# Seven products in place of eight for half of the gate and up projections of a hybrid layer's two feed-forward stages

## The chip, the cores and the metric

The kernel runs on one core of a Trainium2 chip. The time is the device time of one execution in microseconds. Everything is float32 from outside; inside, each operand is split into a high and a low part (fp32r), and a product of two such operands is three matmuls (high by high, high by low, low by high), so that the result keeps float32's precision.

## The reference

One layer of an encoder trunk, on 256 tokens of width 2048: a feed-forward stage, a mixer (retention and a state-space part in parallel) and a second feed-forward stage, each with a scaled residual and a layer norm behind it. The change touches the two feed-forward stages:

```
D_FF = 5632
def swiglu_ffn(x, w_gate, w_up, w_down):
    return (jax.nn.silu(x @ w_gate) * (x @ w_up)) @ w_down

x = layer_norm(DEEPNORM_ALPHA * x + 0.5 * swiglu_ffn(x, ffn1...), ln1_gain, ln1_bias)
mix = hybrid_mixer(x, ...)
x = layer_norm(DEEPNORM_ALPHA * x + mix, ln2_gain, ln2_bias)
x = layer_norm(DEEPNORM_ALPHA * x + 0.5 * swiglu_ffn(x, ffn2...), ln3_gain, ln3_bias)
```

## The kernel before

The 256 tokens are two tiles of 128 (t = 0, 1), the width of 2048 is 16 blocks of 128 (k). Each feed-forward stage has 11 column tiles of 512 (`NH`), j = 0 to 10. For each, `ffn` runs the gate projection and then the up projection: `proj` (line 164) takes four weight units of 1 MB (128x2048, four blocks of k by 512 columns), and for each k and t `mm_t` (line 114) issues three matmuls of 128x512 into a PSUM bank of that t. So a unit is 24 matmuls, and a column tile 2 x 4 x 24 = 192. `gated` (line 237) makes silu(gate) times up times 0.5 (two activations on ScalarE, two operations on VectorE), and `turn` (line 248) transposes the result on TensorE (8 small matmuls) and splits it for the down projection. The down projection (`down`, line 267) comes in chunks of 4, 4 and 3 column tiles (`CHUNKS`): for each of four output tiles n, all units of the chunk go into two banks, which `add_res` (line 262) adds to the residual rows `res` in SBUF. The last chunk ends in the layer norm (`LN.close`).

A weight unit goes through `wparts` (line 91): SP's queue loads `raw`, ScalarE casts it to the high part `hi`, VectorE subtracts to get the low part `lo`. There are 4 buffers for `hi`, 4 for `lo` and 3 for `raw`, and they set how far loads run ahead: a load waits until VectorE has read the raw buffer that it takes.

The first column tile of the first stage (lines 177 to 210) loads tokens and gate and up units together, in smaller pieces, since all of them start cold. The first gate tile of the second stage is run inside the closing of the layer norm before it.

The order in which each engine gets its instructions is set by the framework's scheduler, which works from a timeline of its own; only within the layer norms' closes is the program's order kept (`strict`). `page` (line 56) hands out 27 tiles of 128x512 for activations (`NPG`), `tmp` 12 of 128x256. `rope_tables` (line 521) makes the rotary tables; the scheduler puts its instructions at the program's start.

## Time and profile before

| | |
|---|---|
| median of 3 runs | 1921.06 us (1919.58 to 1921.64) |
| the profiled execution | 1921.3 us |
| its span | 1919.5 us |
| TensorE busy | 1885.5 us, 98% |
| VectorE busy | 1046.7 us, 55% |
| ScalarE busy | 778.2 us, 41% |
| GpSimd busy | 60.9 us, 3% |
| mean granted TensorE clock | 0.995 |
| DMA | 363.07 MB, mean 189 GB/s |

PE is TensorE, PEld its weight loads, DVE VectorE, ACT ScalarE, POOL GpSimd, SP SyncE, which issues the weight loads. The span runs from the first to the last event of the profile; the execution's own time is 1.8 us longer. In the names of tiles, h and l ahead of a weight's name are its high and low part and r is the raw load; f1 and f2 are the two stages, then g, u, d with the numbers of column tile and unit.

### The profile page before, as it was taken

To read this page: it belongs to the slowest core of one execution; us is meant where nothing else is said; L and a number is where in the kernel's file an instruction comes from. 1 tells how busy PE (TensorE), PEld (TensorE's weight loads), DVE (VectorE), ACT (ScalarE), POOL (GpSimd) and SP (SyncE) were. 2 spreads that over 40 slices of the span, in tenths; PEclk is the share of its full clock that TensorE was granted. 3 is DMA by queue.
4 is the path that set the end of the run, shared out by engine and by line. 5 is a ranking of instruction groups with operands and counts; after the bars stand their busy time and mean duration, and the time that the engine had idled before them with its cause. 6 is when DMAs were issued, how large, how long until landed. Compare 5 with 4: busy or idle time off the path is not lost.

```text
span 1919.5 us, 20769 instructions
## 1 busy us (share of the span) xinstructions
PE 1885.5 (98%) x8722; PEld 1566.5 (82%) x8722; DVE 1046.7 (55%) x1044; ACT 778.2 (41%) x672; POOL 60.9 (3%) x72
## 2 busy tenths in 40 slices
PE   8999999999999998999999998999999999999997
PEld 6888888888888887888888886888888888888885
DVE  6444445444444455867867645644445444444456
ACT  5433333433333336653335437433433343333331
POOL 3000000000000000002300000000000000000000
PEclk9999999999999999999999999999999999999999
DMA  8655555555555553544345554555555555556551
GB/s 331 217 186 195 189 187 194 194 183 194 197 192 200 206 200 137 215 174 160 132 156 190 197 198 142 214 187 187 196 194 188 188 198 184 188 197 234 184 196 66
DMA packets 53581, 363.07 MB, mean 189 GB/s; under 512 B 6240, under 2 KB 6512, under 8 KB 10992
## 3 DMA queue, kind: packets, MB, share of 16 engines
q1 hardware_dynamic: 49536, 350.25, 50.8%
q0 software_dynamic: 2656, 9.41, 1.4%
q10 hardware_dynamic: 1296, 2.10, 0.3%
q8 instruction: 68, 1.11, 0.2%
q14 instruction: 25, 0.20, 0.0%
HBM read 359.63 MB, written 2.10 MB: 188 GB/s over the span
## 4 chain that ended last, share of the span: by engine, by line
PE 95%; ACT 2%; DVE 2%; DMA 1%; issue 0%; POOL 0%; SPq 0%; DVEq 0%
PE f2u L78 12%; PE f1g L78 11%; PE f2g L78 11%; PE f1u L78 11%; PE f1d_p L78 9%; PE f2d_p L78 9%; PE opp L78 4%; PE xb L78 3%; PE f1dz_p L78 3%; PE f2dz_p L78 3%; PE g L78 2%; PE z L78 2%; PE first L78 1%; PE v L78 1%; PE v0e L78 1%; DVE res L78 1%
## 5 line engine op out<-in xcount | busy, mean ns | idle before, releaser
L78 PE MATMUL f2u<-hf2u,l2x 128*128 128x512 f32 x704 | 218.8, 389 | 0.0
L78 PE MATMUL f1g<-hf1g,x 128*128 128x512 f32 x640 | 201.5, 391 | 0.0
L78 PE MATMUL f2g<-hf2g,l2x 128*128 128x512 f32 x640 | 201.2, 391 | 0.0
L78 PE MATMUL f1u<-hf1u,x 128*128 128x512 f32 x640 | 198.6, 389 | 0.0
L78 DVE TENSOR_TENSOR lf2u<-rf2u,hf2u 128x2048 fp32r<-128x2048 f32 x44 | 100.9, 2292 | 125.2 <-ACT hf2u L78 125.2
L78 DVE TENSOR_TENSOR lf1u<-rf1u,hf1u 128x2048 fp32r<-128x2048 f32 x40 | 91.7, 2292 | 122.3 <-ACT hf1u L78 122.3
L78 PEld LDWEIGHTS f2u<-hf2u,l2x 128*128 128x128 f32 x704 | 132.1, 188 | 27.3
L78 DVE TENSOR_TENSOR lf1g<-rf1g,hf1g 128x2048 fp32r<-128x2048 f32 x40 | 91.6, 2292 | 101.5 <-ACT hf1g L78 101.5
L78 DVE TENSOR_TENSOR lf2g<-rf2g,hf2g 128x2048 fp32r<-128x2048 f32 x40 | 91.6, 2292 | 98.7 <-ACT hf2g L78 98.7
L78 PEld LDWEIGHTS f1u<-hf1u,x 128*128 128x128 f32 x640 | 120.1, 188 | 24.9
L78 PEld LDWEIGHTS f1g<-hf1g,x 128*128 128x128 f32 x640 | 120.2, 188 | 24.8
L78 PEld LDWEIGHTS f2g<-hf2g,l2x 128*128 128x128 f32 x640 | 120.1, 188 | 24.6
L78 PE MATMUL f2u<-lf2u,l2x 128*128 128x512 f32 x352 | 137.0, 389 | 0.2 <-DVE lf2u L78 0.2
L78 ACT CAST hf2g<-rf2g 128x2048 fp32r<-128x2048 f32 x40 | 76.5, 1913 | 131.4 <-PE f2u L78 98.9
L78 ACT CAST hf2u<-rf2u 128x2048 fp32r<-128x2048 f32 x44 | 84.1, 1911 | 110.6 <-PE f2g L78 104.7
L78 ACT CAST hf1g<-rf1g 128x2048 fp32r<-128x2048 f32 x40 | 76.4, 1913 | 125.0 <-PE f1u L78 95.3
L78 PE MATMUL f1g<-lf1g,x 128*128 128x512 f32 x320 | 124.6, 389 | 0.0
L78 PE MATMUL f2g<-lf2g,l2x 128*128 128x512 f32 x320 | 124.6, 389 | 0.0
L78 PE MATMUL f1u<-lf1u,x 128*128 128x512 f32 x320 | 124.5, 389 | 0.0
L78 DVE TENSOR_TENSOR lf2d<-rf2d,hf2d 128x2048 fp32r<-128x2048 f32 x32 | 73.4, 2293 | 85.6 <-ACT hf2d L78 85.6
L78 DVE TENSOR_TENSOR lf1d<-rf1d,hf1d 128x2048 fp32r<-128x2048 f32 x32 | 73.4, 2293 | 85.6 <-ACT hf1d L78 85.6
L78 ACT CAST hf1u<-rf1u 128x2048 fp32r<-128x2048 f32 x40 | 76.4, 1910 | 106.3 <-PE f1g L78 105.5
(797 smaller groups left out, 3846.4 us busy)
## 6 DMA issues: line engine op xcount, KB each, us to landing
rf2u<-f_u SPq DMA_DIRECT2D x44, 1024.0 KB, 4.8
rf1g<-f_g SPq DMA_DIRECT2D x40, 1024.0 KB, 4.8
rf1u<-f_u SPq DMA_DIRECT2D x40, 1024.0 KB, 4.8
rf2g<-f_g SPq DMA_DIRECT2D x40, 1024.0 KB, 4.8
rf1d<-f_d SPq DMA_DIRECT2D x32, 1024.0 KB, 4.8
rf2d<-f_d SPq DMA_DIRECT2D x32, 1024.0 KB, 4.8
rop<-wout SPq DMA_DIRECT2D x16, 1024.0 KB, 4.8
rf1dz<-f_d SPq DMA_DIRECT2D x12, 1024.0 KB, 4.8
```

The lines of the kernel that those rows point to most:

```text
L78: ins = fn(*args, **kw)
```

## The change

For column tiles 1 to 10 of each stage (20 of 22), the first half of the inner dimension (units 0 and 1 of gate and up, 16 k blocks of which 8) is computed by Strassen's scheme in Winograd's form. The 2 x 2 blocks are: two token tiles by two k halves of the activations (a11, a12, a21, a22) and two k halves by gate and up of the weights (g1, g2, u1, u2). Seven products, each 4 blocks of k by three matmuls = 12 matmuls, take the place of eight. `forms` makes the four combinations of activations once per stage: 12 operations of VectorE and 4 casts on ScalarE, each 128x512. `fused` makes the four sums of weights (u1-g1, u1-u2 kept as u2-u1, u2-g1, g2-u2) per tile on VectorE as 128x2048 operations, and splits seven weight operands in place of four; the other half (units 2 and 3) stays as it was. Four copies on ScalarE keep intermediate sums of a PSUM bank, because bank x goes on accumulating: the first product, then the fourth (t2), then the fifth (t3).

The down projection of tiles 0 to 7 no longer goes by chunks: `rows_at` runs it for one column tile at a time, a unit of 24 matmuls for each n, and the four units stand between the products of the next tile (`more()`). Each unit is added to the residual by itself. Tiles 9 and 10 have no down units between their products; the last down projection has tiles 8, 9 and 10 as before.

Memory: `raw` and `lo` share 6 buffers (4 + 3 before), the Strassen loads have 4 of their own ("sr"), `NPG` is 19, and there is a pool per stage (`phase`) which holds `tmp`, the Strassen loads or the convolution's pages (`page2`). `rope_tables` moves ahead of the first stage in the text. The last layer norm's rows come in two wide loads of 128x2048 in place of eight of 128x512.

```diff
-CHUNKS = [(0, 4), (4, 4), (8, 3)]
+LASTC = 8
-NPG = 27
+NPG = 19
...
+    def page2(name, dt=F32, shape=(P, 512)):
+        return phase["pool"].tile(list(shape), dt, tag="pm", name=name, bufs=9)
...
     def wparts(src, name, k, c):
         n = k * c
         hi = wpool.tile([P, D], F32R, tag="whi", name="h" + name, bufs=4)
-        lo = wpool.tile([P, D], F32R, tag="wlo", name="l" + name, bufs=4)
-        raw = wpool.tile([P, D], F32, tag="raw", name="r" + name, bufs=3)
+        lo = wpool.tile([P, D], F32R, tag="wrl", name="l" + name, bufs=6)
+        raw = wpool.tile([P, D], F32, tag="wrl", name="r" + name, bufs=6)
...
+    cs = const.tile([P, 2, T], F32, name="cs")
+
+    def rope_tables():
...
+    rope_tables()
...
+                r = 2 * self.idx + i
+                src = aps["lnr"][r:r + 1, :]
+                if self.nxt is None:
+                    g = phase["pool"].tile([P, D], F32, tag="sr", name=f"{self.name}gb{i}", bufs=4)
+                    nc.gpsimd.dma_start(out=g, in_=src.broadcast_to([P, D]))
+                    self.gb.append([g[:, n * NS:(n + 1) * NS] for n in range(4)])
+                    continue
                 row = []
                 for n in range(4):
                     g = page(f"{self.name}gb{i}{n}")
-                    r = 2 * self.idx + i
-                    nc.gpsimd.dma_start(
-                        out=g, in_=aps["lnr"][r:r + 1, n * NS:(n + 1) * NS].broadcast_to([P, NS]))
+                    nc.gpsimd.dma_start(out=g, in_=src[:, n * NS:(n + 1) * NS].broadcast_to([P, NS]))
...
-    def ffn(act, which, ln, psg, psu=None):
+    def forms(x4, name):
+        r = {}
+        for q in range(2):
+            for t in range(2):
+                v = page(f"{name}r{q}{t}", F32, (P, 4, P))
+                sl = slice(t * P, (t + 1) * P)
+                vec.tensor_tensor(out=v, in0=x4[q][:, :, 0, sl].bitcast(F32), in1=x4[q][:, :, 1, sl].bitcast(F32),
+                                  op=ALU.add)
+                r[q, t] = v
+        a11, a21, a12, a22 = r[0, 0], r[0, 1], r[1, 0], r[1, 1]
+        vec.tensor_tensor(out=a22, in0=a21, in1=a22, op=ALU.add)
+        vec.tensor_tensor(out=a21, in0=a11, in1=a21, op=ALU.subtract)
+        vec.tensor_tensor(out=a11, in0=a22, in1=a11, op=ALU.subtract)
+        vec.tensor_tensor(out=a12, in0=a12, in1=a11, op=ALU.subtract)
+        out = []
+        for i, v in enumerate((a22, a11, a21, a12)):
+            hi = page(f"{name}sh{i}", F32R, (P, 4, P))
+            lo = page(f"{name}sl{i}", F32R, (P, 4, P))
+            split(v, hi, lo)
+            out.append(lambda k, hi=hi, lo=lo: (hi[:, k, :], lo[:, k, :]))
+        return out
+
+    def ffn(act, x4, which, ln, psg, psu=None):
         wg, wu, wd = aps[f"{which}_g"], aps[f"{which}_u"], aps[f"{which}_d"]
         todo = []
 
@@ -472,31 +547,129 @@
         def run(src, name):
             got = None
             for i, ps in enumerate(proj(src, act, name)):
-                if i == 0:
-                    flush()
                 got = ps
             return got
 
-        pend = None
-        for ci, (j0, nj) in enumerate(CHUNKS):
-            hs = []
-            for j in range(j0, j0 + nj):
-                if psg is None:
-                    psg = run(wg[j], f"{which}g{j}")
-                if psu is None:
-                    psu = run(wu[j], f"{which}u{j}")
-                toks = gated(psg, psu, f"{which}t{j}")
-                todo.append(lambda toks=toks, j=j, hs=hs: turn(toks, f"{which}t{j}", hs))
-                psg = psu = None
-                if pend is not None:
-                    pend()
-                    pend = None
-
-            def pend(hs=hs, nj=nj, j0=j0, ci=ci):
-                down(lambda n, u: wd[n, j0 + u], hs, nj, f"{which}d{ci}_", ci == 0)
+        if psu is None:
+            psu = run(wu[0], f"{which}u0")
+        s1f, s2f, s3f, s4f = forms(x4, which)
+
+        def raw_of(q, t):
+            return lambda k: act[4 * q + k](t)
+
+        def rows_at(j, n, hs):
+            pss = [bank(f"{which}d{j}p{n}{t}") for t in range(2)]
+            w = wunit(wd[n, j], f"{which}d{j}_{n}", 4, NS)
+            for k in range(4):
+                for t in range(2):
+                    mm_t(pss[t], hs[k], t, w, k, k == 0, k == 3)
+            for t in range(2):
+                add_res(pss[t], t, n, j == 0)
+
+        def fused(j, rest):
+            name = f"{which}s{j}"
+            fx = phase["pool"]
+
+            def load(src, nm):
+                t = fx.tile([P, D], F32, tag="sr", name=f"{name}{nm}", bufs=4)
+                nc.sync.dma_start(out=t, in_=src)
+                return t
+
+            def parts(v, nm):
+                hi = wpool.tile([P, D], F32R, tag="whi", name=f"{name}h{nm}", bufs=4)
+                lo = wpool.tile([P, D], F32R, tag="wrl", name=f"{name}l{nm}", bufs=6)
+                split(v, hi, lo)
+                return hi.rearrange("p (k c) -> p k c", c=NS), lo.rearrange("p (k c) -> p k c", c=NS)
+
+            def prod(ps, fm, w, first, last):
+                for k in range(4):
+                    ah, al = fm(k)
+                    ten.matmul(ps, lhsT=ah, rhs=w[0][:, k, :], start=first and k == 0, stop=False, skip_group_check=True)
+                    ten.matmul(ps, lhsT=ah, rhs=w[1][:, k, :], start=False, stop=False, skip_group_check=True)
+                    ten.matmul(ps, lhsT=al, rhs=w[0][:, k, :], start=False, stop=last and k == 3, skip_group_check=True)
+
+            def plain(src, kc, nm, banks, first, last):
+                w = wunit(src[kc], f"{name}{nm}{kc}", 4, NS)
+                for k in range(4):
+                    for t in range(2):
+                        ah, al = act[4 * kc + k](t)
+                        ps = banks[t]
+                        ten.matmul(ps, lhsT=ah, rhs=w[0][:, k, :], start=first and k == 0, stop=False, skip_group_check=True)
+                        ten.matmul(ps, lhsT=ah, rhs=w[1][:, k, :], start=False, stop=False, skip_group_check=True)
+                        ten.matmul(ps, lhsT=al, rhs=w[0][:, k, :], start=False, stop=last and k == 3, skip_group_check=True)
+
+            def more():
+                if rest:
+                    rest.pop(0)()
+
+            def sub(o, a, b):
+                vec.tensor_tensor(out=o, in0=a, in1=b, op=ALU.subtract)
+
+            def snap(ps, nm):
+                v = page(f"{name}{nm}")
+                sca.copy(out=v, in_=ps)
+                return v
+
+            def plus(v, ps):
+                vec.tensor_tensor(out=v, in0=ps, in1=v, op=ALU.add)
+
+            g1 = load(wg[j, 0], "g1")
+            u1 = load(wu[j, 0], "u1")
+            x = bank(name + "x")
+            prod(x, raw_of(0, 0), parts(g1, "g1"), True, True)
+            c11 = snap(x, "c11")
+            b1 = [bank(f"{name}b{t}1") for t in range(2)]
+            plain(wg[j], 2, "g", b1, True, False)
+            u2 = load(wu[j, 1], "u2")
+            sub(g1, u1, g1)
+            yb = bank(name + "y")
+            prod(yb, s1f, parts(g1, "t1"), True, True)
+            c22 = snap(yb, "c22")
+            flush()
+            plain(wg[j], 3, "g", b1, False, False)
+            g2 = load(wg[j, 1], "g2")
+            more()
+            b12 = bank(name + "b12")
+            prod(b12, s4f, parts(u2, "u2"), True, False)
+            sub(u1, u2, u1)
+            sub(u2, u2, g1)
+            prod(x, s2f, parts(u2, "t2"), False, True)
+            c12 = snap(x, "c12")
+            vec.tensor_tensor(out=c12, in0=c12, in1=c22, op=ALU.add)
+            more()
+            prod(x, s3f, parts(u1, "t3"), False, True)
+            c21 = snap(x, "c21")
+            prod(b1[0], raw_of(1, 0), parts(g2, "g2"), False, True)
+            plus(c11, b1[0])
+            sca.activation(c11, c11, AF.Silu)
+            more()
+            sub(g2, g2, u2)
+            prod(b1[1], raw_of(1, 1), parts(g2, "t4"), False, True)
+            plus(c21, b1[1])
+            sca.activation(c21, c21, AF.Silu)
+            plain(wu[j], 2, "u", [b12, x], False, False)
+            more()
+            plain(wu[j], 3, "u", [b12, x], False, True)
+            plus(c12, b12)
+            plus(c22, x)
+            for a, u in ((c11, c12), (c21, c22)):
+                vec.scalar_tensor_tensor(out=a, in0=u, scalar=0.5, in1=a, op0=ALU.mult, op1=ALU.mult)
+            return [c11, c21]
+
+        hs = []
+        toks = gated(psg, psu, f"{which}t0")
+        todo.append(lambda toks=toks, hs=hs: turn(toks, f"{which}t0", hs))
+        rest = [lambda n=n, hs=hs: rows_at(0, n, hs) for n in range(4)]
+        tail = []
+        for j in range(1, NH):
+            toks = fused(j, rest)
+            hs = [] if j <= LASTC else hs
+            todo.append(lambda toks=toks, j=j, hs=hs: turn(toks, f"{which}t{j}", hs))
+            if j < LASTC:
+                rest = [lambda n=n, j=j, hs=hs: rows_at(j, n, hs) for n in range(4)]
         if ln.nxt is None:
             ln.affine()
-        return down(lambda n, u: wd[n, j0 + u], hs, nj, f"{which}dz_", False, ln, flush)
+        return down(lambda n, u: wd[n, LASTC + u], hs, NH - LASTC, f"{which}dz_", False, ln, flush)
 
...
-    ps1 = ffn(act0, "f1", ln1, first_ps[0], first_ps[1])
-    ps2 = mixer(ln1.x, ps1, ln2)
-    ffn([halves(a) for a in ln2.x], "f2", LN(2, "l3"), ps2)
+    with tc.tile_pool(name="fx1", bufs=1) as phase["pool"]:
+        ps1 = ffn(act0, x0_4, "f1", ln1, first_ps[0], first_ps[1])
+    with tc.tile_pool(name="mx", bufs=1) as phase["pool"]:
+        ps2 = mixer(ln1.x, ps1, ln2)
+    with tc.tile_pool(name="fx2", bufs=1) as phase["pool"]:
+        ffn([halves(a) for a in ln2.x], ln2.x4, "f2", LN(2, "l3"), ps2)
```

Three places show what the new order is; the names are f1s4 for the Strassen tile 4 of the first stage (x, y, b01, b11, b12 its banks; c11 to c22 its copies; ht2 and lt2 the parts of u2-g1, ht3 and lt3 those of u2-u1), f1d3_0 to f1d3_3 for the four down units of column tile 3, which stand between its products, and f1t3 for that tile's transposed result.

ScalarE before, in the gate and up units of tile 5, where the casts alternate with little else:

```order
L78 CAST hf1g53_2119<-rf1g53_2121 128x2048 [waits DMAHW0_49,DVE_49,PE_49]
L78 CAST hf1u50_2151<-rf1u50_2153 128x2048 [waits DMAHW1_49,DVE_49,PE_49]
L78 CAST f1t4h0_2046<-f1t4T0_2041 128x512 [waits PE_49]
L78 CAST f1t4h1_2055<-f1t4T1_2050 128x512 [waits PE_49]
L78 CAST hf1u51_2181<-rf1u51_2183 128x2048 [waits DMAHW2_49,DVE_49,PE_49]
L78 CAST hf1u52_2211<-rf1u52_2213 128x2048 [waits DMAHW3_49,DVE_49,PE_49]
```

ScalarE now, in the middle of Strassen tile 4:

```order
L83 CAST f1s4ht2_1940<-f1s4u2_1815 128x2048 [waits DVE_49,Activation_49]
L83 CAST hf1d3_1_1961<-rf1d3_1_1963 128x2048 [waits DMAHW1_49,PE_49,Activation_49]
L83 COPY f1s4c12_1956<-f1s4x_1764 128x512 [waits PE_49]
L83 CAST f1s4ht3_1993<-f1s4u1_1762 128x2048 [waits Activation_49]
L83 CAST f1s4hg2_2011<-f1s4g2_1885 128x2048 [waits DMAHW2_49]
L83 CAST hf1d3_2_2031<-rf1d3_2_2033 128x2048 [waits DMAHW2_49,DVE_49]
```

A cast no longer stands behind loads and buffers only: the copy c12, which waits for TensorE's fourth product in bank x, stands between two of them. The same order stands in tiles 1 to 8 of both stages.

TensorE now, from the fourth product's last matmul on:

```order
L83 MATMUL f1s4x_1764<-f1s4ht2_1940,f1sl1_483 128x512
L83 MATMUL f1d3p10_1959<-hf1d3_1_1961,f1t3h0_1842 128x512 [waits Activation_49]
L83 MATMUL f1d3p11_1960<-hf1d3_1_1961,f1t3h0_1842 128x512 [waits PE_49]
L83 MATMUL f1s4x_1764<-f1s4ht3_1993,f1sh2_486 128x512 [waits Activation_49]
L83 MATMUL f1d3p10_1959<-lf1d3_1_1962,f1t3h0_1842 128x512 [waits DVE_49]
L83 MATMUL f1d3p10_1959<-hf1d3_1_1961,f1t3l0_1843 128x512
```

Two matmuls of the down unit, one of the fifth product, then the other 22 of the down unit.

SP now, from the first load for tile 5 on:

```order
L575 DMA f1s5g1_2180<-f1_g 128x2048 [waits DMAHW0_49,DVE_49,Activation_49]
L101 DMA rf1d3_1_1963<-f1_d 128x2048 [waits DMAHW1_49,PE_49]
L101 DMA rf1d3_2_2033<-f1_d 128x2048 [waits DMAHW5_49,DMAHW2_49,PE_49]
L575 DMA f1s5u1_2182<-f1_u 128x2048 [waits DMAHW3_49,DVE_49]
L575 DMA f1s5u2_2235<-f1_u 128x2048 [waits DVE_49]
L101 DMA rf1s4u2_2084<-f1_u 128x2048 [waits DMAHW7_49,PE_49]
```

Loads for the next tile and for the down units of this one alternate, and the queue takes them in this order.

## Rows read from the trace of the kernel before

**Rows 1.** The page: span, busy time of each engine, and the chain that ended last.

```profile
span 1919.5 us, 20769 instructions
PE 1885.5 (98%) x8722; PEld 1566.5 (82%) x8722; DVE 1046.7 (55%) x1044; ACT 778.2 (41%) x672; POOL 60.9 (3%) x72
...
PE 95%; ACT 2%; DVE 2%; DMA 1%; issue 0%; POOL 0%; SPq 0%; DVEq 0%
```

**Rows 2.** TensorE's waits: what it waited for, us in total, times, longest.

```profile
PE first L78 <- ACT hfirstg L78: 7.3, 2, 5.8
PE l2T L78 <- ACT res L78: 5.3, 3, 3.8
```

**Rows 3.** Busy times by stretch: 100 us inside the first feed-forward stage.

```profile
core 0: us, PE busy (x) PEld busy (x) DVE busy (x) ACT busy (x) POOL busy (x), PEclk, DMA share, GB/s
300.00:400.00 100.00, 100.00 (x450) 82.94 (x449) 46.63 (x27) 38.52 (x26) 0.00 (x0) 1.00 0.52 190
```

**Rows 4.** Timeline of TensorE in an up tile: start, us, instructions, idle before.

```profile
77.39 0.39 PE L78 MATMUL f1u<-hf1u,x 128*128 128x512 f32 x1
...
88.72 0.61 PE L78 MATMUL f1u<-hf1u,x 128*128 128x512 f32 x2
```

**Rows 5.** The page's groups: count, busy, mean ns of one, idle before and releaser.

```profile
L78 DVE TENSOR_TENSOR lf1u<-rf1u,hf1u 128x2048 fp32r<-128x2048 f32 x40 | 91.7, 2292 | 122.3 <-ACT hf1u L78 122.3
L78 ACT CAST hf1u<-rf1u 128x2048 fp32r<-128x2048 f32 x40 | 76.4, 1910 | 106.3 <-PE f1g L78 105.5
L78 DVE SCALAR_TENSOR_TENSOR res<-res,f1d_p 128x512 f32<-128x512 f32 x16 | 10.9, 688 | 4.2 <-PE f1d_p L78 4.2
```

**Rows 6.** Timeline of VectorE in the mixer: operations back to back.

```profile
781.43 4.90 DVE L78 TENSOR_TENSOR res<-res,l1gb 128x512 f32<-128x512 f32 x8
786.25 4.49 DVE L78 TENSOR_TENSOR lxb<-rxb,hxb 128x2048 fp32r<-128x2048 f32 x2
```

**Rows 7.** Timeline of ScalarE: two copies of 128x512 out of PSUM.

```profile
326.98 1.06 ACT L78 CAST f1t4h<-f1t4T 128x512 fp32r<-128x512 f32 x2
```

**Rows 8.** DMA issues, median us to landing: the whole program, then 36 to 37 us.

```profile
rf1u<-f_u SPq DMA_DIRECT2D x40, 1024.0 KB, 4.8
...
rf1g<-f_g SPq DMA_DIRECT2D x1, 1024.0 KB, 7.5
```

**Rows 9.** Waits of SP's queue.

```profile
SPq L96 <- DVE lf1u L78: 209.5, 40, 6.0
```

**Rows 10.** Timelines at the start: TensorE, then VectorE.

```profile
27.81 0.50 PE L78 MATMUL first<-lfirstu,x 128*128 128x512 f32 x1 [0.81 <-DVE lfirstu L78]
...
26.72 0.43 DVE L78 SCALAR_TENSOR_TENSOR th<-n,th 128x256 f32<-128x256 f32 x1 [1.23 <-POOL n L534]
```

**Rows 11.** TensorE around three waits: stretches (columns as rows 3), then timeline.

```profile
756.00:761.00 5.00, 4.65 (x16) 3.93 (x17) 0.70 (x2) 3.80 (x8) 0.00 (x0) 0.66 0.26 111
1170.00:1174.00 4.00, 3.72 (x19) 2.87 (x20) 2.59 (x6) 3.22 (x8) 0.00 (x0) 1.00 0.70 262
1180.80:1186.50 5.70, 5.63 (x16) 4.63 (x17) 0.69 (x1) 3.56 (x8) 0.00 (x0) 0.52 0.20 83
...
756.35 1.09 PE L78 MATMUL l1T<-ident,res 128*128 128x128 f32 x4 [3.81 <-issue]
757.09 0.78 PE L78 MATMUL v0e<-hv,l1x 128*128 128x512 f32 x1
760.90 0.40 PE L78 MATMUL v0e<-hv,l1x 128*128 128x512 f32 x1
1170.08 0.66 PE L78 MATMUL l2T<-ident,res 128*128 128x128 f32 x4 [1.28 <-ACT res L78]
1180.87 1.11 PE L78 MATMUL l2T<-ident,res 128*128 128x128 f32 x4 [3.77 <-ACT res L78]
1181.63 0.78 PE L78 MATMUL f2se<-hf2s,l2x 128*128 128x512 f32 x1
1186.41 0.39 PE L78 MATMUL f2se<-hf2s,l2x 128*128 128x512 f32 x1
```

More of the change, by code (lines that the diff above doesn't have):

```diff
@@ L57, in page @@
         return pages.tile(list(shape), dt, tag="pg", name=name, bufs=NPG)
+    phase = {}
     def tmp(name, dt=F32, shape=(P, T)):
-        return tmps.tile(list(shape), dt, tag="t1", name=name, bufs=12)
+        return phase["pool"].tile(list(shape), dt, tag="t1", name=name, bufs=12)
+    def page2(name, dt=F32, shape=(P, 512)):
+        return phase["pool"].tile(list(shape), dt, tag="pm", name=name, bufs=9)
     def small(name, shape, dt=F32):
@@ L185, in tile_layer @@
             hi = wpool.tile([P, D], F32R, tag="whi", name=f"hfirst{nm}{kc}", bufs=4)
-            lo = wpool.tile([P, D], F32R, tag="wlo", name=f"lfirst{nm}{kc}", bufs=4)
-            raws.append(wpool.tile([P, D], F32, tag="raw", name=f"rfirst{nm}{kc}", bufs=3))
+            lo = wpool.tile([P, D], F32R, tag="wrl", name=f"lfirst{nm}{kc}", bufs=6)
+            raws.append(wpool.tile([P, D], F32, tag="wrl", name=f"rfirst{nm}{kc}", bufs=6))
             ws.append((hi, lo))
@@ L228, in tile_layer, with nround, msub @@
         tc.keep_in_program_order(nc.gpsimd.dma_start(out=res[t], in_=aps["x"][t]))
+    cs = const.tile([P, 2, T], F32, name="cs")
+    def rope_tables():
+        pos_i = page("pos_i", I32, (P, T))
+        nc.gpsimd.dma_start(out=pos_i, in_=aps["pos"].broadcast_to([P, T]))
+        th = page("th", F32, (P, T))
+        nc.gpsimd.tensor_copy(out=th, in_=pos_i)
+        nc.gpsimd.tensor_scalar(out=th, in0=th, scalar1=invf, scalar2=None, op0=ALU.mult)
+        MAGIC = 12582912.0
+        p1 = _split(TWO_PI * 4096.0, 7, 6)
+        q2 = _split(TWO_PI, 12, 3)
+        def nround(src, scale, name):
+            r = page(name, F32, (P, T))
+            nc.gpsimd.tensor_scalar(out=r, in0=src, scalar1=scale, scalar2=MAGIC, op0=ALU.mult, op1=ALU.add)
+            nc.gpsimd.tensor_scalar(out=r, in0=r, scalar1=-MAGIC, scalar2=None, op0=ALU.add)
+            return r
+        def msub(dst, n, c, src):
+            vec.scalar_tensor_tensor(out=dst, in0=n, scalar=-c, in1=src, op0=ALU.mult, op1=ALU.add)
+        n1 = nround(th, 1.0 / (TWO_PI * 4096.0), "n1")
+        for c in p1[:3]:
+            msub(th, n1, c, th)
+        ta = page("ta", F32, (P, T))
+        msub(ta, n1, float(np.float32(sum(p1[3:]))), th)
+        n2 = nround(ta, 1.0 / TWO_PI, "n2")
+        msub(th, n2, q2[0], th)
+        msub(th, n1, p1[3], th)
+        msub(th, n2, q2[1], th)
+        msub(th, n1, p1[4], th)
+        msub(th, n2, q2[2], th)
+        msub(th, n1, p1[5], th)
+        PI_LO = 3.1415925
+        nc.gpsimd.tensor_scalar(out=th, in0=th, scalar1=PI_LO, scalar2=-PI_LO, op0=ALU.min, op1=ALU.max)
+        sca.activation(cs[:, 1, :], th, AF.Sin)
+        vec.scalar_tensor_tensor(out=ta, in0=th, scalar=-1.0, in1=th, op0=ALU.mult, op1=ALU.max)
+        nc.gpsimd.tensor_scalar(out=ta, in0=ta, scalar1=-1.0, scalar2=float(np.float32(np.pi / 2)),
+                                op0=ALU.mult, op1=ALU.add)
+        sca.activation(cs[:, 0, :], ta, AF.Sin)
+    rope_tables()
     def group_f(units, xT, name):
@@ L569, in tick @@
                 fn(*args)
-        conv = [page(f"conv{i}", F32, (P, 2, T)) for i in range(6)]
+        conv = [page2(f"conv{i}", F32, (P, 2, T)) for i in range(6)]
         def conv_block(b, ps):
@@ L582, in conv_block @@
             sca.activation(conv[b // 2][:, b % 2, :], o, AF.Silu, bias=par[:, 48 + b:49 + b])
-        rope_tables()
         wdr = page("wdr", F32, (P, KD, SH))
```

36 lines of the change are left out of this document (removed).

## The prediction

> **What bounds the kernel now.** I read the page's busy times first: TensorE is busy in 98% of the span, VectorE in 55%, ScalarE in 41%, and 95% of the chain that ended last is TensorE's [rows 1]. TensorE's waits are next: the two largest add up to 7.3 and 5.3 us, at the start and in the second layer norm [rows 2]. In the steady part of a feed-forward stage there are none: a 100 us stretch is 100% busy at full clock [rows 3]. So a matmul that disappears there is time that disappears, until another engine is late. Its price comes from TensorE's timeline: from the start at 77.39 to the one at 88.72 lie 50 matmuls of 128x512, so one takes 11.33 / 50 = 0.2267 us (the 389 ns of one record is its latency) [rows 4]. The helpers are not short of time: VectorE waits 122 us for ScalarE's casts in one of the groups alone [rows 5].
>
> **What the change removes.** In the 20 Strassen tiles, half of the inner dimension takes 7 products of 12 matmuls in place of 8: 84 for 96, 12 fewer per tile. 20 x 12 x 0.2267 = 54.4 us come off TensorE's work. The transposes, the down matmuls, the mixer and the layer norms keep theirs. The profiled run took 1921.3 us, 0.2 above the median of the runs shown; 1921.3 - 54.4 = 1866.9 would be the time if nothing waited.
>
> **What it adds to VectorE and ScalarE.** Per Strassen tile VectorE gets four weight sums and three more subtractions of 128x2048, at 2.29 us each alone [rows 5] and 2.20 apart when back to back (4.49 for two) [rows 6], and some small ones at 0.60 apart (4.90 for eight) [rows 6]. The down units by column tile add 48 additions into the residual per stage (72 for 24), 0.69 us each [rows 5]. A tile's part is 7 x 2.29 + 5 x 0.69 = 19.5 us, and with the forms' 24 operations (17 us) it is 20 x 19.5 + 96 x 0.69 + 17 = 473 us in all: VectorE goes from 1047 [rows 1] to some 1520 us. ScalarE gets three casts of 1.91 and four copies out of PSUM of 0.53 each (1.06 for two [rows 7]) per tile, some 157 us in all. Neither becomes the busiest. Of the 20 tiles, 16 have down units between the products ("ordinary"): 276 matmuls, 62.6 us, with 19 big and 17 small VectorE operations, 19 x 2.20 + 17 x 0.60 = 52.0 us. Four have none ("bare", tiles 9 and 10 of each stage): 180 matmuls, 40.8 us, with 15 big and 9 small, 38.4 us. So cover is enough in the ordinary tile by sums and thin in the bare one; what costs is order.
>
> **The wait in the ordinary tile.** The order of the change shows it. On ScalarE the copy c12 out of bank x, which must wait for the last matmul of the fourth product, stands directly before the cast of the fifth product's weights (ht3). On TensorE two matmuls of the down unit follow the fourth product, and then comes the fifth product's first matmul, which waits for ht3; the other 22 of the down unit stand behind it. From the start of the last matmul of the fourth product: 0.39 to its end [rows 4], 0.04 to ScalarE, 0.53 for the copy [rows 7], 1.91 for the cast [rows 5], 0.05 back to TensorE: 2.92 us. TensorE would have gone on after 3 x 0.2267 = 0.68. So it waits 2.24 us, in 16 tiles: **35.8 us back**. The two short hops are the gaps between neighbouring records, and leaving them out moves the sum by 1.4 us. Everything queued behind ht3 on ScalarE (hg2, the next down cast) moves with it, as TensorE does.
>
> **Other tight places.** Placing the ordinary tile by hand with these durations, the next ones are the second gate unit's low part at the start of a tile and the low parts of the last up and down units, all within 0.05 us of their use. I take 0.04 per tile, 0.6 in all; at the other end is rival 2. In the bare tile three chains are short of cover: sum, cast, subtraction, product, for t2, t3 and t4, each with 2.20 + 1.91 + 2.20 before its product, and only 12 to 24 matmuls (2.7 to 5.4 us) in between. Below, nothing waits (0). Above, I get 0.95 + 0.6 + 2.2 = 3.75 us a tile by the back-to-back durations. I take 2.7, nearer the upper end, since those are the rows nearest to it: the bare tile just breaks even, and **10.8 us go back** over four.
>
> **The ends of the stages.** At the start of the first stage, 4 MB of Strassen loads go out ahead of the start's later units, and loads that queue up there took 7.5 us from issue to landing against 4.8 in the steady part [rows 8]. On the other side the wait of 0.81 us at 27.81, where VectorE had stood behind GpSimd's rope rounding [rows 10], may go. The first stage's forms (12 operations on VectorE, 12 x 0.69 = 8 us) also come before the first tile. I bound this at -1 to +5 and take +2, the middle. At the start of the second stage VectorE has the layer norm's 16 affine operations (9.6 us), the forms and the first units together: -1 to +5; I take +1, as TensorE has the rest of the first up tile there, 96 matmuls or 21.8 us. The LN3 rows by two wide transfers instead of eight, and the pools by stage, cost nothing: the last down products cover them, 288 matmuls or 65 us.
>
> **SP's queue.** The number of bytes is unchanged, and the queues moved 190 GB/s at half of their share [rows 3]. What changes is what SP waits for: the load of the next tile's g1 stands behind VectorE's sum that frees its buffer, and the down and up units stand behind that load. I cost it at nothing, since a tile's 12 MB have 66 us; rival 2 is the case where that fails.
>
> **Sum:** 1921.3 - 54.4 + 35.8 + 0.6 + 10.8 + 2 + 1 = **1917.1 us**. A measurement of this kernel tells 0.2% (3.8 us) from no change, so this lies at the edge between faster and the same. An ordinary tile gains 2.72 - 2.24 - 0.04 = 0.44 us; a bare one nothing.
>
> **Rivals.**
> 1. *The bare tiles and the ends cost nothing.* VectorE's waits in the trace [rows 5] say that there is room; the chains above say there isn't. Without these terms: 1917.1 - 10.8 - 3 = **1903 us**, with half of them 1910.
> 2. *The chain of VectorE, SP, DMA, ScalarE binds in the ordinary tile.* SP sends the next g1 only after a sum on VectorE, with a down unit directly behind; the second of two close loads lands after 7.5 us, not 4.8 [rows 8], and VectorE's 19 big operations at 2.29 instead of 2.20 add 1.7 us to a chain with 0.05 us to spare. Then a tile takes 1.5 us more than I have it: 1917.1 + 16 x 1.5 = **1941 us**. It decides once the chain is later by 0.05 us. Against it: the loads are spread, and SP waits for VectorE 209 us in one group now [rows 9] with TensorE full.
> 3. *TensorE's clock falls after the waits* (slower). [...] After the 3.81 us at 756.35 it was 0.66, and 12 v0e matmuls started over 3.81 us (757.09 to 760.90), +1.3 [rows 11]. [...] If each such wait brings the low clock, 16 x (1.3 to 2.3) = 21 to 37 us: **1938 to 1954 us**. [...]
>
> That the change does less than it says is excluded by its order: the products stand there with 12 matmuls each.
>
> **How the numbers follow.** Forecast (1910 to 1926) 0.40; rival 1 0.25, its price being bounded by rows; rival 3 0.20, as the idle time lies between rows of both kinds; rival 2 0.15. Of the forecast's 0.40, some 0.19 is below 1917.2, 0.15 within 0.2%, 0.06 above. Faster: 0.19 + 0.25 = 0.44; the same 0.15; slower 0.06 + 0.20 + 0.15 = 0.41. The range begins at 1897: rival 1 with the ends at -1 each (-2), the short hops out (-1.4) and a matmul's modelled end 0.16 us earlier in each wait (0.39 against the pitch of 0.23, -2.6). It ends at 1948: rival 2 with both ends at their upper bounds (+7), and the lower two thirds of rival 3. The forecast's own range is 1910 to 1926.
>
> **What would show it.** In the profile after: in each ordinary tile one idle time of 2.2 us on TensorE, before the fifth product and put down to ScalarE's ht3, 16 in all, some 36 us; in the bare tiles waits for t2, t3 and t4 of 2 to 4 us per tile; granted clock 1.00 in these stretches. TensorE's busy time falls by 54 us. Wrong would be: idle times put down to DMA or to VectorE in ordinary tiles (rival 2), a clock below 1 after each wait (rival 3), or hardly any idle time in the bare tiles (rival 1).

## The result, and the profile after

The changed kernel takes **2026.5 us** (median of 4 runs, 2024.55 to 2029.0) against 1921.35: ratio 1.055, interval 1.0532 to 1.0568. It is 105 us slower. The forecast was 1917.1, its range 1897 to 1948: wrong in sign and size. The profiled execution took 2029.0 us, its span is 107.7 us longer than before. The page of the changed kernel answers to [rows 1] and [rows 8]:

```profile
span 2027.2 us, 20751 instructions
PE 1901.7 (94%) x8482; PEld 1548.8 (76%) x8482; DVE 1480.5 (73%) x1404; ACT 933.8 (46%) x821; POOL 58.4 (3%) x66
...
L83 ACT CAST hf1d<-rf1d 128x2048 fp32r<-128x2048 f32 x32 | 61.1, 1910 | 87.0 <-DMA rf1d<-f_d 87.0
...
rf1d<-f_d SPq DMA_DIRECT2D x32, 1024.0 KB, 6.8
```

TensorE issues the 240 matmuls less, yet is busy 16 us longer, and idle 125.5 us where it was 34.0. So of the 107.7 us, -54.4 is the work, +91.5 idle time, and +70.6 is time in which it was busy with matmuls that took longer. The mean granted clock is 0.966 in place of 0.995: by (1 - clock) x span 69 us are lost to it in place of 10. VectorE and ScalarE are about as busy as forecast (1480.5 us for some 1520, 933.8 for 935). New in the page is the wait of the down units' casts for DMA, 87.0 us in the first stage and 82.6 in the second, with 6.8 us from issue to landing against 4.8.

TensorE's waits by tile (total, times, longest) answer to [rows 2]; single rows for the kinds that repeat:

```profile
PE first L83 <- ACT hfirstg L83: 13.4, 3, 5.9
PE l2T L83 <- ACT res L83: 7.9, 2, 5.4
...
PE f1s9b L83 <- DVE f1s9lt L83: 2.3, 1, 2.3
...
PE f1d4p L83 <- ACT hf1d L83: 2.2, 1, 2.2
...
PE f1s4x L83 <- ACT f1s4ht L83: 1.8, 1, 1.8
```

Added up over the tiles: ht3 25.7 us in 16 waits, casts of down units 17.4 in 9, the start 13.4 in 3, lt4 in the bare tiles 9.5 in 4, low parts of their up units 8.0 in 4. (lt4 is the low part of g2-u2; the views leave the numbers at the ends of names out, so f1s9lt can be lt2, lt3 or lt4 of tile 9.) Where the time went, by first and last matmuls of the stretches (in the second stage the tiles count from the end of tile 0):

| stretch | forecast | measured |
|---|---|---|
| 16 ordinary tiles, 66.2 us each before | -7.0 | +46.6 (69.1 each) |
| 4 bare tiles, 44.45 each before | 0 | +29.9 (51.9 each) |
| start, to the first Strassen tile | +2 | +10.6 |
| last down products, mixer, layer norms, end | +1 | +20.6 |

In the ordinary tiles, where 43.5 us of work were removed, TensorE is now idle for 49.3 us and loses 32.5 us to the clock, by (1 - clock) x time; in the bare tiles it is 23.0 and 13.6 us. Before, both were 0 in these tiles.

**An ordinary tile.** The middle of tile 5 of the first stage, from the timelines of VectorE, ScalarE, TensorE and SP (start, us, instruction, idle before):

```profile
361.39 2.29 DVE L83 TENSOR_TENSOR f1s5u<-f1s5u,f1s5g 128x2048 f32<-128x2048 f32 x1
...
363.74 0.33 SPq L575 DMA_DIRECT2D f1s6g<-f_g  x1
364.17 3.21 SPq L101 DMA_DIRECT2D rf1d<-f_d  x2
...
371.11 1.90 ACT L83 CAST hf1d<-rf1d 128x2048 fp32r<-128x2048 f32 x1 [5.43 <-DMA rf1d<-f_d]
...
372.92 0.58 ACT L83 COPY f1s5c<-f1s5x 128x512 f32<-128x512 f32 x1
...
373.06 0.73 PE L83 MATMUL f1d4p<-hf1d,f1t4h 128*128 128x512 f32 x2 [2.17 <-ACT hf1d L83]
...
373.39 1.90 ACT L83 CAST f1s5ht<-f1s5u 128x2048 fp32r<-128x2048 f32 x1
...
375.35 0.79 PE L83 MATMUL f1s5x<-f1s5ht,f1sh 128*128 128x512 f32 x1 [1.55 <-ACT f1s5ht L83]
```

SP's wait ahead of the first of these loads (us in total, times, longest):

```profile
SPq L575 <- DVE f1s5u L83: 19.0, 1, 19.0
```

Read it from the top. VectorE's sum u2-g1 (the buffer of g1 holds u1-g1 by then) ends at 363.68, and only then may SP send the next tile's g1 into that buffer; SP has waited 19.0 us for it. The down unit d1 stands behind that load, goes out at once after it, at 364.17, and is cast at 371.11. TensorE has finished the fourth product, waits 2.17 us for this cast, runs two matmuls, and waits another 1.55 for ht3 (the cast at 373.39, behind the copy c12), which was forecast to be the only wait.

**The clock behind these waits.** Stretches of 6 us from the fifth product's first matmul on, in tiles 2, 4 and 5 (columns as rows 3, PEclk is the granted clock):

```profile
167.85:173.85 6.00, 6.00 (x26) 4.99 (x27) 5.96 (x4) 3.58 (x2) 0.00 (x0) 1.00 0.35 117
304.99:310.99 6.00, 6.00 (x19) 4.78 (x20) 5.97 (x4) 3.56 (x2) 0.00 (x0) 0.72 0.37 124
375.35:381.35 6.00, 6.00 (x14) 4.74 (x15) 5.96 (x4) 3.55 (x2) 0.00 (x0) 0.50 0.34 113
```

TensorE is busy throughout, with 26, 19 or 14 matmuls. Where both waits were long (8 of 16 tiles, tile 5 is one) the clock fell every time, to 0.50 to 0.76; behind an ht3 wait alone or nearly so (1.55 to 1.85 us) it fell in 4 of 8, to 0.72. In 7 of the first 8 a wait of 0.6 to 0.8 us for lt2 stands 5 us ahead as well, so the two waits are not quite alone there. Summed over the 16 stretches, (1 - clock) x 6 is 27 us.

**A bare tile.** Tile 9 of the first stage, the same timelines:

```profile
643.78 5.33 SPq L575 DMA_DIRECT2D f1s10u<-f_u  x2
...
649.22 0.37 SPq L101 DMA_DIRECT2D rf1s9u<-f_u  x1
...
653.58 0.50 PE L83 MATMUL f1s9b<-f1s9lt,x 128*128 128x512 f32 x1 [2.25 <-DVE f1s9lt L83]
...
656.29 1.90 ACT L83 CAST hf1s9u<-rf1s9u 128x2048 fp32r<-128x2048 f32 x1 [4.30 <-DMA rf1s9u<-f_u]
...
660.83 0.50 PE L83 MATMUL f1s9b<-lf1s9u,x 128*128 128x512 f32 x1 [1.85 <-DVE lf1s9u L83]
```

The tile's own up unit stands on SP behind loads u1 and u2 of the *next* tile, whose buffers VectorE frees late. The wait for lt4 (2.25) was forecast, the one for the up unit's low part (1.85) was not.

**The start.** DMA issues from 20 to 36 us (median us to landing), then TensorE:

```profile
rfirstg<-f_g SPq DMA_DIRECT2D x2, 1024.0 KB, 18.7
...
39.23 1.22 PE L83 MATMUL first<-hfirstg,x 128*128 128x512 f32 x2 [5.10 <-ACT hfirstg L83]
```

With 4 MB of Strassen loads ahead, a load takes 18.7 us where [rows 8] has 7.5; in the run that sends these four behind the start's own loads (below), TensorE's waits for hfirstg are 5.8 us in place of 13.4.

### The profile page after: what moved, and what is told of

Same layout as the page of the kernel before. It is cut to its first block, busy times and chain, and to the rows that moved or that the text cites. A ratio compares the mean times of both kernels' runs of the same rounds, so it can differ in the third digit from the quotient of the medians.

```text
span 2027.2 us, 20751 instructions
## 1 busy us (share of the span) xinstructions
PE 1901.7 (94%) x8482; PEld 1548.8 (76%) x8482; DVE 1480.5 (73%) x1404; ACT 933.8 (46%) x821; POOL 58.4 (3%) x66
## 5 line engine op out<-in xcount | busy, mean ns | idle before, releaser
L83 ACT CAST hf1d<-rf1d 128x2048 fp32r<-128x2048 f32 x32 | 61.1, 1910 | 87.0 <-DMA rf1d<-f_d 87.0
L83 ACT CAST hf2d<-rf2d 128x2048 fp32r<-128x2048 f32 x32 | 61.1, 1911 | 82.6 <-DMA rf2d<-f_d 82.6
L83 PE MATMUL opp<-hop,mx 128*128 128x512 f32 x256 | 80.3, 393 | 1.3 <-ACT hop L83 1.3
L83 PE MATMUL xb<-l1x,hxb 128*128 128x512 f32 x192 | 68.0, 398 | 0.0
L83 PEld LDWEIGHTS opp<-hop,mx 128*128 128x128 f32 x256 | 48.6, 190 | 11.8 <-ACT hop L83 1.7
L83 DVE TENSOR_TENSOR lop<-rop,hop 128x2048 fp32r<-128x2048 f32 x16 | 36.2, 2287 | 25.1 <-ACT hop L83 25.1
L83 PE MATMUL xb<-l1x,lxb 128*128 128x256 f32 x192 | 54.0, 281 | 0.0
L83 PE MATMUL opp<-lop,mx 128*128 128x512 f32 x128 | 50.8, 397 | 2.8 <-DVE lop L83 2.8
L83 PE MATMUL g<-l1x,hg 128*128 128x512 f32 x128 | 45.2, 397 | 0.0
L83 PE MATMUL z<-hz,l1x 128*128 128x512 f32 x128 | 40.5, 394 | 0.0
L83 PE MATMUL first<-hfirstg,x 128*128 128x512 f32 x64 | 25.2, 462 | 13.4 <-ACT hfirstg L83 13.4
L83 DVE TENSOR_TENSOR lxb<-rxb,hxb 128x2048 fp32r<-128x2048 f32 x12 | 27.5, 2291 | 4.0 <-ACT hxb L83 3.9
```

The source lines that it names most:

```text
L83: ins = fn(*args, **kw)
```

## The experiments

Times are medians; the kernel before is at 1920.4 to 1921.4 beside each group of runs. Theory: waits in the order of the queues cost the time, with the clock behind them. Rivals: VectorE's added load, the shared buffers by themselves, the start.

**Is it ht3?** Its cast is put ahead of c12, the fifth product behind the whole down unit.

```diff
-            prod(x, s2f, parts(u2, "t2"), False, True)
-            c12 = snap(x, "c12")
+            w2 = parts(u2, "t2")
+            wd1 = unit_at(*rest[0][:2]) if rest else None
+            w3 = parts(u1, "t3")
+            prod(x, s2f, w2, False, True)
+            c12 = page(f"{name}c12")
+            tc.keep_in_program_order(sca.copy(out=c12, in_=x))
...
-            more()
-            prod(x, s3f, parts(u1, "t3"), False, True)
+            more(wd1)
+            strict[0] = True
+            prod(x, s3f, w3, False, True)
+            strict[0] = False
```

> Edit: in each Strassen tile the cast ht3 is queued on ScalarE ahead of the copy c12, and the fifth product follows the whole of its down unit on TensorE. Theory (the waits come from the order, and the low clock comes from the waits): the 16 waits for ht3 (25.7 us in the profile of the changed kernel) go, and with them part of the low clock, 1 to 2 us a tile; the 9 waits for the first down cast stay. 2027 - 26 - (16 to 32), so 1970 to 1985 us. Rival (VectorE at 73% is late whatever the order): the wait moves to another operand, less than 10 us gained, over 2017 us.

2020.6 us, only 6 better: the theory's number missed, and the time is what the rival had (over 2017). The ht3 waits are gone, but TensorE's waits now show the down unit in their place (here tiles 5 and 4; all 16 have such a wait):

```profile
PE f1d4p L83 <- ACT hf1d L83: 2.5, 1, 2.5
...
PE f1d3p L83 <- DVE lf1d L83: 2.2, 2, 1.6
```

Together 45.2 us in 29 waits, against 19.0 in 11. The unit's load is late in any case; ht3 hid part of that. Whether VectorE's load is behind it, this run can't tell; the runs with the late load moved and with other buffers can.

**The bare tiles.** Tiles 9 and 10 go back to eight products.

```diff
-            toks = fused(j, rest)
+            if j <= LASTC:
+                toks = fused(j, rest)
+            else:
+                toks = gated(run(wg[j], f"{which}g{j}"), run(wu[j], f"{which}u{j}"), f"{which}t{j}")
```

> Edit: column tiles 9 and 10 of both stages run by eight products as before the change; the 16 ordinary tiles keep the seven. Theory: the bare tiles take 52 to 57 us where 44.5 were needed, so 4 x 8 to 12 = 32 to 48 us come back, 1980 to 1995 us. My prediction's term (bare tiles break even) expects no difference, 2027 us.

2002.55 us, 24 better, less than the 32 to 48 expected. From the end of tile 8's products to the last down products it takes 89.1 us in place of 104.0: each bare tile cost 7.5 us *more* than eight products. The ordinary tiles took 7.5 us more in this run (4.6 less in the first stage, 12.1 more in the second).

**Waiting or working?** Nine useless matmuls into a free bank behind the fourth product of the ordinary tiles; c12 and ht3 are held in their order.

```diff
+            if rest:
+                strict[0] = True
+                for i in range(9):
+                    ten.matmul(yb, lhsT=act[0](0)[0], rhs=x4[0][:, 0].rearrange("p a b -> p (a b)"),
+                               start=True, stop=True, skip_group_check=True)
+                strict[0] = False
```

> Edit: nine useless matmuls (2.04 us) into a bank that is free by then stand on TensorE between the fourth product and the down unit of the ordinary tiles, with ScalarE's order as in the changed kernel. More work, no wait removed. Theory of the clock: TensorE no longer stands idle in the wait for ht3, so the clock stays up after it: 16 x (1 to 2.5) = 16 to 40 us faster, 1987 to 2011 us, in spite of 33 us of added work. Rival (the slow matmuls after a wait come from elsewhere, such as operands that are late): no gain, 2027 us, or up to 33 us slower where the work does not fit into the wait.

2021.33 us: 16 x 9 x 0.2267 = 33 us of added work make it 5 us *faster*, at a clock of 0.979; 16 to 40 were expected. The ordinary tiles of both stages, first in the changed kernel, then here:

```profile
65.33:620.82 555.49, 528.91 (x2275) 429.05 (x2274) 420.02 (x285) 260.12 (x185) 0.00 (x0) 0.97 0.49 184
1291.95:1841.67 549.72, 527.04 (x2274) 427.88 (x2273) 425.48 (x289) 259.34 (x185) 0.00 (x0) 0.97 0.49 184
...
64.30:604.73 540.43, 532.71 (x2347) 432.26 (x2345) 420.14 (x285) 259.45 (x185) 0.00 (x0) 1.00 0.50 189
1283.81:1826.44 542.63, 534.40 (x2346) 433.23 (x2345) 426.02 (x289) 259.85 (x185) 0.00 (x0) 1.00 0.50 186
```

There the gain is 22 us: the useless matmuls stand where TensorE waited, and the clock stays at 1.00. SP's order (compared in tiles 2 to 7) is the same, ScalarE's and VectorE's differ in a few places. The bare tiles, which get no such matmuls but the same order of c12 and ht3, have a new wait of 2.5 us each for a cast, take 55.5 us in place of 51.9 and eat 15 of the 22. That the waits' cost is more than their idle time was the point, and the ordinary tiles show it.

**The start.** Tile 1's loads go behind all loads of the start.

```diff
-                nc.sync.dma_start(out=t, in_=src)
+                if which == "f1" and j == 1:
+                    with tc.issue_after(last_first.ins):
+                        nc.sync.dma_start(out=t, in_=src)
+                else:
+                    nc.sync.dma_start(out=t, in_=src)
```

> Edit: the four Strassen loads of tile 1 in the first stage are issued after the start's own loads, as the code stands, not ahead of its third chunk. Theory: the first 192 matmuls end at 65.3 us instead of 54.7 because rfirstg2 lands late behind 4 MB; with the loads moved this wait of 5.1 us goes, and 5 to 10 us come back, 2017 to 2022 us. Rival (the forms and the smaller pools cause it): no change, or the wait moves to the first Strassen tile.

2023.72 us, just outside the 2017 to 2022 expected. The start's first waits go (5.8 us left of 13.4) and tile 1 begins 14 us earlier, but tile 8 ends at 621.0, where it ended at 620.6 in the changed kernel: the tiles of the first stage take 71.0 us each in place of 69.4, with 32.7 us idle in place of 26.6, and eat the lead.

**The late down unit.** The load of the next tile's g1 is issued behind that of d1. The scheduler, working from the new order, then also puts ht3 and hg2 ahead of c12, and moves a few other instructions of ScalarE and VectorE.

```diff
-                nc.sync.dma_start(out=t, in_=src)
+                if nm == "g1" and 1 < j <= LASTC:
+                    with tc.issue_after(raw_dma[f"{which}d{j - 2}_1"].ins):
+                        nc.sync.dma_start(out=t, in_=src)
+                else:
+                    nc.sync.dma_start(out=t, in_=src)
```

> Edit: the load of the next tile's g1 is issued after that of the second down unit (rf1d.._1), not ahead of it; the scheduler, told so, also puts ht3 and hg2 ahead of c12 on ScalarE. Theory (the down unit's load stands on SP behind a load that waits for VectorE's u2-g1): TensorE's waits for the second down cast (17.4 us in 9 tiles in the changed kernel) and for ht3 (25.7 us in 16) go, with the low clock after them; 2027 - 43 - (20 to 40), so 1945 to 1965 us. Rival (VectorE's load): waits reappear for a low part, under 15 us gained, over 2012 us.

1943.6 us, 83 better, 1.4 under the range. Ordinary tiles take 64.4 us: d1 goes out 17.4 us into tile 5 in place of 27.5, the waits for the down units' casts are gone and ht3's are 3.6 us in 2. The ordinary tiles are idle for 7.8 us in place of 49.3, which is 41.5 of the 75 us that they gained; with the same work in them, the other 33.5 are about the 32.5 that they lost to the clock in the changed kernel. The mean granted clock of the whole execution is 0.986 in place of 0.966. The bare tiles are nearly as dear as they were (lt4 9.6 us in 4). As ht3 alone brought 6 us, the rest needs the load's new place; that place with c12 still ahead of ht3 was not run.

**Buffers of their own.** 2 for raw and 4 for low parts in place of 6 shared, the same memory.

```diff
-        lo = wpool.tile([P, D], F32R, tag="wrl", name="l" + name, bufs=6)
-        raw = wpool.tile([P, D], F32, tag="wrl", name="r" + name, bufs=6)
+        lo = wpool.tile([P, D], F32R, tag="wlo", name="l" + name, bufs=4)
+        raw = wpool.tile([P, D], F32, tag="raw", name="r" + name, bufs=2)
```

> Edit: raw loads get 2 buffers and low parts 4 of their own, in place of 6 shared ones; memory is the same, nothing else in the text is changed, the scheduler's order follows. Theory (a raw load takes a shared buffer that TensorE frees late, so loads wait for TensorE and the order comes out as it did): the down units' loads run ahead, the waits of the ordinary tiles mostly go, 1945 to 1970 us; the bare tiles stay dear. Rival (VectorE's load decides): no change, 2020 us or over.

**1897.35 us**, ratio 0.9876 (0.9847 to 0.9905), 48 us under the expected range. Page, then two stretches (a steady one, and the bare tiles), then SP in tile 5:

```profile
PE 1842.8 (97%) x8482; PEld 1527.2 (81%) x8482; DVE 1476.4 (78%) x1404; ACT 935.2 (49%) x821; POOL 59.9 (3%) x66
...
L83 ACT CAST hf1d<-rf1d 128x2048 fp32r<-128x2048 f32 x32 | 61.3, 1916 | 16.3 <-DMA rf1d<-f_d 15.4
```

```profile
300.00:400.00 100.00, 100.00 (x451) 82.94 (x450) 83.44 (x59) 50.38 (x37) 0.00 (x0) 1.00 0.53 196
577.00:661.00 84.00, 83.63 (x375) 68.61 (x374) 70.25 (x44) 47.45 (x37) 0.00 (x0) 1.00 0.38 141
```

```profile
327.52 3.02 SPq L101 DMA_DIRECT2D rf1d<-f_d  x2
337.96 0.33 SPq L575 DMA_DIRECT2D f1s6g<-f_g  x1
```

The scheduler's order changed with the buffers: the down units go out 10 us ahead of g1, ht3 stands before c12, and the bare tile's up units before the next tile's loads. An ordinary tile takes 63.5 us, a bare one 42.3. VectorE does the same work (1476 us, 83% of the steady stretch) with TensorE 100% busy: its load is not the cause by itself.

**Shared buffers alone.** The kernel before, with the 6 shared buffers.

```diff
-        lo = wpool.tile([P, D], F32R, tag="wlo", name="l" + name, bufs=4)
-        raw = wpool.tile([P, D], F32, tag="raw", name="r" + name, bufs=3)
+        lo = wpool.tile([P, D], F32R, tag="wrl", name="l" + name, bufs=6)
+        raw = wpool.tile([P, D], F32, tag="wrl", name="r" + name, bufs=6)
```

> Edit to the kernel BEFORE: raw loads and low parts share 6 buffers as in the changed kernel, in place of 3 + 4; no Strassen product. Theory: the mixer of the changed kernel is 13 us longer (786.4 to 1230.4 us, against 733.6 to 1164.3) because of the shared buffers, and the start too; so 1930 to 1940 us. Rival (the mixer's smaller pages or the moved tables do it): within 3 us of 1921.

1929.11 us, ratio 1.0039 (1.0024 to 1.0055): 0.9 under the range, 8 us slower, 5.0 in the mixer and 1.5 in each of the last down products. The changed kernel loses 20.6 in these parts (13.2 of it in the mixer), so some two fifths of that come with the shared buffers and the order that they lead to.

**The order by hand,** once with buffers of their own, once with the 6 shared ones. All four queues of tiles 1 to 8 are written out; tiles 9 and 10 have eight products. The place that matters, in the order of the text, which each engine keeps:

```diff
+            rd[1] = rload(wd[1, j - 1], S("d1"))
+            rd[2] = rload(wd[2, j - 1], S("d2"))
...
+                q["g1"] = srload(wg[n, 0], nm(n, "g1"))
...
+            hi = cast(u1, S("t3"))
...
+            prod(x, s2f, wt2, False, True)
+            hi = cast(g2, S("g2"))
+            wg2 = low(g2, hi, S("g2"))
+            c12 = page(S("c12"))
+            sca.copy(out=c12, in_=x)
```

> Edit: tiles 1 to 8 of both stages with all four queues in an order written by hand, in which every cast, sum and load stands 4 us or more ahead of its use (next tile's first weights are prepared inside the tile); raw 2 and low 4 buffers of their own; tiles 9 and 10 by eight products. Theory (order and buffers, not VectorE's load, cost the time): an ordinary tile takes 63.5 us for 66.2 before, 16 x 2.7 = 43 us off; with the mixer's and the start's loss of 10 to 20 us left, 1885 to 1905 us. Rival (VectorE at 52 us per 63 us tile can't keep up): a tile stays at 66 us or more, over 1925 us.

> Edit to the hand-ordered kernel: raw loads and low parts share 6 buffers, as in the changed kernel, in place of 2 + 4; the order on all queues is the same. If it is the order that decides: 1903 us, at most 10 more. If the shared buffers by themselves do: loads wait for TensorE to free a low part, waits for casts come back in most tiles, over 1925 us.

1903.04 us, within its range, and 1897.19, not slower but 6 us faster. Both run ordinary tiles from tile 2 on in 63.5 us, and with 6 shared buffers the steady stretch is again full:

```profile
300.00:400.00 100.00, 100.00 (x451) 83.02 (x450) 84.79 (x58) 50.18 (x35) 0.00 (x0) 1.00 0.49 179
```

So the shared buffers cost nothing in the tiles by themselves. They mattered because the scheduler made its order from them.

**The forecast's own wait, alone.** The hand order, with only c12 back before ht3 and the fifth product's first matmul behind three of the down unit's (two in the changed kernel); then the same with nine useless matmuls. The first two lines marked + belong to the first run, the last pair to the second.

```diff
+            c12 = page(S("c12"))
+            sca.copy(out=c12, in_=x)
             hi = cast(u1, S("t3"))
...
-            for i in range(0):
+            for i in range(9):
                 ten.matmul(yb, lhsT=act[0](0)[0], rhs=x4[0][:, 0].rearrange("p a b -> p (a b)"),
```

> Edit to the hand-ordered kernel (1903 us, no waits in its ordinary tiles): c12 stands ahead of ht3 on ScalarE again, and the fifth product's first matmul stands after three matmuls of the down unit, so that only the wait of my prediction comes back, about 2.0 to 2.2 us in each of 16 tiles. My term alone: 1903 + 32 to 36 = 1935 to 1939 us. Theory of the clock: a wait of this length brings the low clock in some tiles, 1 to 2.5 us more in half or more of them, so 1945 to 1975 us.

> Edit to the previous kernel: nine useless matmuls (2.04 us) on TensorE ahead of the down unit, so that the wait for ht3 is filled with work. Without an effect of the wait on the clock the two are equal, 1935 to 1940 us both. With it this one stays there and the previous one is 10 to 35 us slower than this.

1944.27 us against 1903.04 (0.7 under the range), and 1932.5 with the wait filled. TensorE in tiles 2 and 3 of the kernel with the wait, and the 6 us behind each:

```profile
158.67 0.50 PE L83 MATMUL f1s2x<-hf1s2t,f1sh 128*128 128x512 f32 x1 [1.79 <-ACT hf1s2t L83]
...
224.21 0.50 PE L83 MATMUL f1s3x<-hf1s3t,f1sh 128*128 128x512 f32 x1 [1.79 <-ACT hf1s3t L83]
```

```profile
158.67:164.67 6.00, 6.00 (x26) 4.99 (x27) 6.00 (x4) 3.57 (x2) 0.00 (x0) 1.00 0.46 146
224.21:230.21 6.00, 6.00 (x19) 4.79 (x20) 6.00 (x4) 3.56 (x2) 0.00 (x0) 0.72 0.41 145
```

The same wait of 1.79 us stands in all 16 tiles. In 11 the clock stays up (1.00 in tile 2), and from tile 2 on such a tile takes 65.5 us, 2.0 more than 63.5; in 5 it falls (to 0.72 in tile 3) and the tile takes 67.1. The wait was sized well: with three matmuls ahead in place of two the forecast's sum gives 2.24 - 0.23 = 2.01, and 2.0 were paid. The clock adds 1.6 us in about a third: 11 x 2.0 + 5 x 3.6 = 40 of the 41 us. Filled with work, every tile from tile 2 on takes 65.6 us, the 63.5 and the 9 x 0.2267 of added work. The whole is 11.8 us faster than to wait (13.3 in the profiled executions), but only 7.7 us of that lie in tiles 2 to 8; most of the rest is in tile 1 of each stage, where another wait, for the low part of f1t0 and f2t0, is shorter (0.7 and 1.5 us in place of 3.3 and 2.6).

**The best of these.** Own buffers, tile 1's loads behind the start's, and the mixer's state copies early.

```diff
+                if which == "f1" and j == 1:
+                    with tc.issue_after(last_first.ins):
+                        nc.sync.dma_start(out=t, in_=src)
...
-            sca.copy(out=st[g], in_=pS)
+            tc.keep_in_program_order(sca.copy(out=st[g], in_=pS))
...
-        at(11, ssd_decay, 0, 0)
         at(11, ssd_state, 0)
-        at(12, ssd_decay, 0, 1)
+        at(11, ssd_decay, 0, 0)
         at(12, ssd_state, 1)
+        at(12, ssd_decay, 0, 1)
```

> Edit to the kernel with buffers of its own for raw loads and low parts (1897 us): the Strassen loads of tile 1 go behind the start's own, and the mixer's two state copies ahead of the decay activations on ScalarE. Theory: 8 to 11 us at the start (first 192 matmuls end at 68.6 us, 54.7 before) and 4 to 7 us from the mixer's two waits for the state (4.4 us and the clock after them); 1880 to 1886 us. Rival: the waits move, over 1892 us.

1896.43 us, ratio 0.9873 (0.9857 to 0.989): no better than own buffers alone, and what the rival had (over 1892). The start is 11 us shorter, but tile 1 takes 69.2 in place of 63.5, and the mixer 3.6 more: the waits moved. TensorE's waits:

```profile
PE py L83 <- DVE sx L83: 4.4, 2, 2.9
...
PE pi L83 <- ACT sx L83: 2.9, 2, 1.8
PE f1s1b L83 <- ACT hf1s1g L83: 2.5, 1, 2.5
```

With own buffers alone, one of TensorE's waits in the mixer is this:

```profile
PE pi L83 <- ACT st L83: 4.4, 2, 2.2
```

Some 25 of the 54.4 us can be had by these versions. With own buffers alone the 20 tiles give 51.5; 13.9 go back at the start, 4.7 between the mixer and the second stage's tile 1, and 9.5 in the mixer, where TensorE waits these 4.4 us for state copies (pi) that cost it nothing before, and loses 6.8 us to the clock where it lost 1.7. How to have these parts as short as before was not found; which of their waits come from the Strassen loads and which from the memory given to them stays open.

## Why the prediction was wrong

**Right.** *The removed matmuls.* With a fitting order the steady stretch is 100% busy and a tile takes 63.5 us, which is 276 x 0.2267 and the transposes. *VectorE and ScalarE are not the bound*: busy times came out within 3%. *The ht3 wait*: in all 16 tiles, 25.7 us recorded for 35.8 forecast (the wait for d1 takes part of it), and 2.0 us each where it was put back alone. "What costs is order" was right too; it was followed through for ScalarE and TensorE only.

**The step that failed first is SP's queue**: "I cost it at nothing, since a tile's 12 MB have 66 us". That is an average of bytes. What counts is the head of the queue: in tile 5 the g1 load waits there 19.0 us for VectorE's sum, and d1 stands behind it, though nothing more holds it once g1 is out. The order shown ahead of the prediction has the row (g1, then d1, d2), and the prediction named it, but the sum u2-g1 was not placed in time against d1's use. With this trace's times that gives 364.2 for the d1 load, 6.9 us until its cast begins, 1.9 for the cast: 373, and TensorE was there 2.2 us earlier. Rival 2 held this chain, at 1.5 us a tile and 0.15; its argument against ("the loads are spread") was the same average. Undoing it, with the new order that followed from it (ht3's place above all), brought 83 us.

**Bare tiles: break even was wrong by 7.5 us each.** The t4 chain was seen; that the tile's up units stand on SP behind the next tile's loads was not. It is the same error at a second place. Per bare tile lt4 cost 2.4 us of the 2.7 forecast for all three chains, the up unit another 2.5, and the clock, which the forecast left out, 3.4. In good order the bare tile takes 42.3 us and gains 2.

**The clock was a rival and should have been a term.** The rows had no fall at 1.28 us idle and one at 3.77 [rows 11]; 2.24 lay between, and I put the forecast on the lower side. Rival 3's price of 1.3 to 2.3 us a wait is in these rows too: behind idle times of 3.81 and 3.77 us, 12 matmuls started over 3.81 and 4.78 us, where 11 x 0.2267 = 2.49 is the pace at full clock. Measured: alone, a wait of 1.79 us lowered the clock in 5 of 16 tiles, for 1.6 us each; single waits of 1.55 to 1.85 us in the changed kernel, in 4 of 8; two waits with two matmuls between, in 8 of 8.

**The ends: +3 forecast, +31 measured.** The bound for the start came from a landing time of 7.5 us [rows 8] with few loads waiting; with 4 MB ahead it was 18.7. I had taken the mixer and the layer norms as untouched, though the diff changes their buffers; the kernel before with 6 shared buffers shows 8 us for that.

**The range.** The rivals were treated as cases that exclude each other. Here rivals 2 and 3 came together: where the late load makes a second wait, the clock came down each time (8 of 8 tiles). Ordinary tiles alone came out 16 x 3.35 = 54 us above forecast, the bare ones 30, the ends 28; the upper end allowed 31 in all. The observations that I named as "wrong" (waits put down to DMA, a clock below 1) are the ones that came.

## What to carry to other kernels

Where a change adds loads to an in-order queue, place each load's release (the operation that frees its buffer) against the need of every load behind it; bytes per stage say nothing on that. Where a scheduler makes the order, shared buffers and new loads move instructions far from the edit, so a saving in arithmetic that comes out slower may only want another order: here the same products run at 2027 or 1897 us. Price a wait of some 2 us on TensorE with its clock (here 2.0 us, and 3.6 in 5 of 16 tiles), and rivals with a common cause as a sum.
